# Prompt attention of a hybrid encoder step: all softmax steps of a pair of heads at the scheduling priority of the masked maximum

## Chip, cores, metric

The kernel runs on one core of one Trainium2 chip. The metric is the device time of one execution in microseconds. The kernel before took 1340.0 us, the median of 3 runs (1339.12 to 1340.05).

## What is computed

Two layers of a streaming encoder step, for a prompt of 512 rows and a sample of 32 rows behind 1024 cached positions. Both share the weights. Model width is 1024, float32. What the change concerns is mixer C of a layer: attention in which each query sees only the keys that an indexer selects. Cut to that:

```python
def sparse_attend(q, qi, wi, k_all, v_all, ki_all, limit, k_top):
    logits = jax.nn.relu(jnp.einsum('bqnd,bsd->bqns', qi, ki_all).astype(jnp.float32))
    iscore = jnp.einsum('bqn,bqns->bqs', wi.astype(jnp.float32), logits)
    admissible = jnp.arange(S)[None, :] < limit[:, None]
    iscore = jnp.where(admissible[None], iscore, -jnp.inf)
    _, sel = lax.top_k(iscore, k_top)
    ...
    s = jnp.einsum('bqhgd,bqkhd->bqhgk', qg, k_sel).astype(jnp.float32) * (HEAD_DIM ** -0.5)
    s = jnp.where(valid[:, :, None, None, :], s, -jnp.inf)
    p = jax.nn.softmax(s, axis=-1)
    o = jnp.einsum('bqhgk,bqkhd->bqhgd', p.astype(v_sel.dtype), v_sel)

def layer(...):
    z = rms_norm(x, g_mix) @ w_in
    y_a = spatial gating of za (gelu, 128-row chunks);  y_b = short gated convolution of zb
    y_c = sparse_attend of q, k, v (8 heads, 4 key heads, 64 wide; 128 keys of the prompt, 256 of the sample)
    x = x + concat(y_a, y_b, y_c) @ w_out
    x = x + square(relu(rms_norm(x) @ w_up)) @ w_down
```

## The kernel before

Everything is unrolled Python, one loop over the two layers. The prompt's rows are four blocks of 128 (b = 0 to 3), the sample's 32 rows the fifth (b = 4). A float32 product runs as three matmuls of parts (L258, L259, L260: high by high, low by high, high by low); weights are fetched on the SP queue, cast to the high part on ScalarE (L226), and the low part is the difference, on VectorE or POOL (L227).

A layer goes: indexer projection and scores, Q, K and V projections (`tok_gemm`, with `tok_gemm` of block 4 taken from small products on 32 rows, L428, and summed by L421), then attention and the other mixers, the output projection, the feed-forward part. Program order in the attention part is: the search for the sample's 256 keys (`sample_mask`: sixteen digits, each a counting pass on ScalarE, L490, small VectorE steps, and a one-column matmul, L493), `attend(0)`, then for b = 1, 2, 3 the top-128 mask (`topk_mask`: 16 rounds of MAX8, L465, and MATCH_REPLACE, L466, on 256, 384 or 512 columns; L467 turns the result into a mask) and `attend(b)`, then `mixers()`, then `attend_sample()`. Mixer A takes its V half in five products (the first uses L428 too), a gelu each on ScalarE (L908), and a spatial product each (L897).

`attend(b)` handles four pairs of heads. For a pair: two score products into PSUM tiles `psl` (L762; there are two such tiles); for each head, the masked maximum, which reads the scores and the mask and writes the masked scores and their maximum (L770, VectorE); the bias (L771, one column, VectorE); Exp with its sum (L772, ScalarE); the reciprocal (L773, one column, VectorE); the scaling (L775 on ScalarE for b below 2, L777 on VectorE otherwise). Then the probabilities are transposed (L106 into `psx` or `psd`), copied out of PSUM (L790) and multiplied by V (L794 into `pso`).

The order on each engine isn't the program's. A scheduler takes the instructions by priority, which is their place in the program plus an offset, as their inputs and buffers come free in its own reckoning. `with evac:` lowers the number of what stands in it by 2000000, `with prep:` by 1000000, so that such instructions come ahead of all others that are ready:

```python
PREP = -1000000
EVAC = -2000000

class Shift:
    def __enter__(self):
        self.tc.cur_priority += self.off
```

Each engine then runs its list strictly in that order. Before the change only L770 of the softmax steps stands in `with evac:`; the masks' rounds and the search's digits have no offset. In names such as `t_1840` the number is that of the tile; psl_1833 and psl_1834 are the scores of the second pair of heads of block 0 in layer 0, 1861 the third, 1888 the fourth, 1965, 1996, 2028 and 2059 the pairs of block 1.

Of the kernel before, what the change touches and what calls it, by code (L numbers as in the profile page):

```python
# [11 lines left out]
AF = mybir.ActivationFunctionType  # L12
ALU = mybir.AluOpType
# [42 lines left out]
def kernel(  # L56
# [7 lines left out]
    nc = tc.nc  # L64
# [16 lines left out]
    def T(n, tag=None):  # L81
        return tp.tile([128, n], F32, tag=tag or "t", name=nm("t"), bufs=TBUFS[tag or "t"])
# [4 lines left out]
    def sm(n, tag, bufs=4):  # L87
        return sp.tile([128, n], F32, tag=tag, name=nm(tag), bufs=bufs)
# [3 lines left out]
    def by_turns():  # L92
        turn[0] += 1
        return "xd"[turn[0] % 2]

    def psum(tag):
        return pp.tile([128, 512], F32, tag=tag, name=nm("ps" + tag), bufs=PBUFS[tag])

    def keep(shape, tag, dt=F32, bufs=1):
        return main.tile(shape, dt, tag=tag, name=nm(tag), bufs=bufs)  # L100

    def tr(out, in_, ident):

        if in_.dtype == F32R:
            out = out.bitcast(F32R)
        nc.tensor.transpose(out, in_, ident)  # L106
# [146 lines left out]
    def split(hi, lo, src):  # L253
        nc.scalar.copy(hi, src)
        nc.vector.tensor_tensor(lo, src, hi.bitcast(F32), op=ALU.subtract)
# [135 lines left out]
    for l in range(depth):  # L391
# [267 lines left out]
        rq = [keep([128, 8], f"rq{b}") for b in range(5)]  # L659
# [92 lines left out]
        def attend(b):  # L752

            hb, off = BLK[b]
            n = 128 * (b + 1)

            def scores(u, hh):

                p = [psum("l"), psum("l")]
                for j in range(2):  # L760
                    e = slice(64 * j, 64 * j + 64)
                    nc.tensor.matmul(p[j][:, :n], lhsT=qT[b][e, u, hh, :], rhs=kTp[e, u, :n], start=True, stop=True)  # L762
                ss2, mx, nb = sm(2, "sa", 6), sm(2, "sa", 6), sm(2, "sa", 6)
                probs = []
                for j in range(2):
                    c = 4 * u + 2 * j + hh
                    o = slice(j, j + 1)
                    t = T(n, "tt")
                    with evac:
                        nc.vector.tensor_tensor_reduce(out=t, in0=p[j][:, :n], in1=masks[b], op0=ALU.add, op1=ALU.max, scale=1.0, scalar=-3e38, accum_out=mx[:, o])  # L770
                    nc.vector.scalar_tensor_tensor(nb[:, o], mx[:, o], -1.0, rq[b][:, c:c + 1], op0=ALU.mult, op1=ALU.mult)  # L771
                    nc.scalar.activation(t, t, AF.Exp, bias=nb[:, o], scale=rq[b][:, c:c + 1], accum_out=ss2[:, o])  # L772
                    nc.vector.reciprocal(ss2[:, o], ss2[:, o])  # L773
                    if b < 2:
                        nc.scalar.activation(t, t, AF.Copy, scale=ss2[:, o])  # L775
                    else:
                        nc.vector.tensor_scalar(t, t, ss2[:, o], None, op0=ALU.mult)  # L777
                    probs.append(t)
                return probs

            def values(u, hh, probs, po):
                for k0 in range(0, b + 1, 2):
                    kn = min(2, b + 1 - k0)
                    pt = psum(by_turns() if b >= 2 else "x")
                    for k in range(kn):
                        for j in range(2):
                            tr(pt[:, (2 * k + j) * 128:(2 * k + j + 1) * 128], probs[j][:, (k0 + k) * 128:(k0 + k + 1) * 128], idn)
                    t = T(NT + NS, "pt")
                    with evac:
                        nc.scalar.copy(t[:, :kn * 256], pt[:, :kn * 256])  # L790

                    for k in range(kn):
                        for j in range(2):
                            nc.tensor.matmul(po[64 * j:64 * j + 64, hh * 128:hh * 128 + 128], lhsT=Vp[:, k0 + k, (2 * u + j) * 64:(2 * u + j + 1) * 64],  # L794
                                             rhs=t[:, (2 * k + j) * 128:(2 * k + j + 1) * 128], start=(k0 + k == 0), stop=(k0 + k == b))
                if hh == 1:
                    dst = [ys[hb][i][:, 4 + 2 * u:6 + 2 * u, off:off + 128] for i in range(2)]
                    split(dst[0], dst[1], po[:, :256].rearrange("p (h t) -> p h t", h=2))

            po = None  # L800
            for u in range(2):
                for hh in range(2):
                    probs = scores(u, hh)
                    if hh == 0:
                        po = psum("o")
                    values(u, hh, probs, po)
# [170 lines left out]
        else:  # L977
            p = psum("x")
            tr(p[:8 * depth, :128], convout.rearrange("p l c -> p (l c)"), idn)
            t = T(128)  # L980
# [46 lines left out]
        for c in range(4):  # L1027
# [12 lines left out]
            for fs in groups:  # L1040
# [5 lines left out]
                for h, n in enumerate(HALF):  # L1046
                    for f, w in zip(fs, ws):
                        p = fm_gemm(h, hs, w)
                        t = hidden[f][:, 256 * h:256 * h + n]
# [169 lines left out]
```

## Time and profile before

| | |
|---|---|
| median of the runs | 1340.0 us |
| profiled execution | 1342.9 us, span 1341.1 us |
| TensorE (PE) busy | 1299.7 us, 97% of the span |
| VectorE (DVE) busy | 1062.6 us, 79% |
| ScalarE (ACT) busy | 750.5 us, 56% |
| POOL busy | 103.8 us, 8% |
| mean granted TensorE clock | 0.981 of full |

The profile is one execution. Busy time of TensorE is the union of its pipelined matmuls. Its clock has two levels, 2.4 GHz and 1.2 GHz; the granted clock of a window is the mean over it, 1.00 where it is at full speed and 0.50 at the lower level. A wait is the idle time of an engine just before an instruction, put down to the instruction that released it. In rows of the timeline, each has its start, its duration, and how many instructions were merged.

### The profile page before, as it was taken

Reading aid. Unit: us, or ns where it says so; the run is one execution under the profiler, and the core shown is the slowest. Engines: PE = TensorE matmul, PEld = TensorE weight load, DVE = VectorE, ACT = ScalarE, POOL = GpSimd, SP = SyncE. Lnnn points to the kernel's source line nnn. Section 1 sums busy time; section 2 is a strip of 40 time slices with the busy share of each in tenths; the row PEclk is TensorE's granted clock in tenths of the full one; section 3 lists DMA queues with packets and bytes.
Section 4 is the critical chain, followed back from the end, with each engine's and each line's share of the span. In section 5 each row is a group of like instructions: output and inputs, shape, how many; then the busy total and the mean of one; then the engine's idle time right before and its main releaser. Section 6 shows DMA issues by size and latency. Waiting matters only on the chain.

```text
span 1341.1 us, 25813 instructions
## 1 busy us (share of the span) xinstructions
PE 1299.7 (97%) x10054; PEld 1212.9 (90%) x10056; DVE 1062.6 (79%) x2585; ACT 750.5 (56%) x1496; POOL 103.8 (8%) x109
## 2 busy tenths in 40 slices
PE   7898999999999999999998999999999999999998
PEld 6777887799999999999986888778999999999997
DVE  6899997567976967958989989774879588597695
ACT  5656885555535535446655579662564454463552
POOL 5215100001000000000021110000200000000000
PEclk7998999999999999999989999999999999999999
DMA  7125213032233232332211222122232423323221
GB/s 210 33 74 123 60 54 123 17 92 79 80 112 94 79 110 79 95 111 68 84 50 60 72 73 81 56 63 74 75 99 64 122 69 95 111 79 109 91 85 68
DMA packets 150802, 113.00 MB, mean 84 GB/s; under 512 B 7028, under 2 KB 147848, under 8 KB 150680
## 3 DMA queue, kind: packets, MB, share of 16 engines
q1 hardware_dynamic: 148040, 106.35, 26.4%
q0 software_dynamic: 2640, 5.01, 1.8%
q8 instruction: 79, 1.29, 0.4%
q14 instruction: 43, 0.35, 0.1%
HBM read 106.67 MB, written 4.67 MB: 83 GB/s over the span
## 4 chain that ended last, share of the span: by engine, by line
PE 81%; DVE 10%; issue 3%; DMA 3%; ACT 2%; POOL 0%; POOLq 0%; SPq 0%; DVEq 0%; ACTq 0%
PE psm L258 16%; PE psm L259 15%; PE psm L260 15%; PE psl L1086 13%; PE psd L1086 6%; PE pso L1086 3%; PE psl L762 2%; PE psx L106 2%; PE pso L794 2%; PE psd L106 1%; DVE work L623 1%; DMA ahi<-in_x_prompt_dram 1%; DMA raw<-in_w_down_dram 1%; DVE work L466 1%; PE psl L653 1%
## 5 line engine op out<-in xcount | busy, mean ns | idle before, releaser
L226 ACT CAST hi<-raw 128x1024 fp32r<-128x1024 f32 (+1 forms) x124 | 126.7, 1023 | 123.7 <-PE psm L259 71.2
L259 PE MATMUL psm<-h1lo,hi 128*128 128x288 f32 x640 | 190.5, 298 | 0.0
L258 PE MATMUL psm<-h1hi,hi 128*128 128x288 f32 x640 | 190.3, 297 | 0.0
L260 PE MATMUL psm<-h1hi,lo 128*128 128x288 f32 x640 | 189.5, 296 | 0.0
L227 DVE TENSOR_TENSOR lo<-raw,hi 128x1024 fp32r<-128x1024 f32 (+1 forms) x99 | 118.6, 1200 | 81.7 <-ACT hi L226 81.4
L258 PE MATMUL psm<-h0hi,hi 128*128 128x256 f32 x640 | 181.9, 284 | 0.0
L260 PE MATMUL psm<-h0hi,lo 128*128 128x256 f32 x640 | 181.0, 283 | 0.5 <-POOL lo L227 0.5
L259 PE MATMUL psm<-h0lo,hi 128*128 128x256 f32 x640 | 181.2, 283 | 0.0
L1086 PE MATMUL psl<-e,hi 128*128 128x272 f32 x768 | 151.4, 290 | 1.2 <-DVE x L1079 0.8
L1086 PEld LDWEIGHTS psl<-e,hi 128*128 128x128 f32 x768 | 121.6, 189 | 3.4 <-DVE x L1079 1.2
L258 PEld LDWEIGHTS psm<-h1hi,hi 128*128 128x128 f32 x640 | 120.3, 188 | 2.4 <-issue 2.3
L260 PEld LDWEIGHTS psm<-h0hi,lo 128*128 128x128 f32 x640 | 120.6, 188 | 1.0 <-POOL lo L227 0.9
L258 PEld LDWEIGHTS psm<-h0hi,hi 128*128 128x128 f32 x640 | 120.6, 188 | 0.7 <-issue 0.5
L259 PEld LDWEIGHTS psm<-h1lo,hi 128*128 128x128 f32 x640 | 120.3, 188 | 0.9 <-issue 0.8
L260 PEld LDWEIGHTS psm<-h1hi,lo 128*128 128x128 f32 x640 | 120.6, 188 | 0.4 <-issue 0.3
L259 PEld LDWEIGHTS psm<-h0lo,hi 128*128 128x128 f32 x640 | 120.5, 188 | 0.3 <-issue 0.2
L243 ACT CAST hi<-t 128x512 fp32r<-128x512 f32 x128 | 78.4, 619 | 70.5 <-PE psl L1086 24.2
L227 POOL TENSOR_TENSOR lo<-raw,hi 128x1024 fp32r<-128x1024 f32 (+1 forms) x25 | 58.1, 2325 | 734.2 <-ACT hi L226 718.0
L1086 PE MATMUL psl<-e,lo 128*128 128x272 f32 x384 | 111.0, 289 | 0.0
L243 ACT CAST hi<-raw 128x512 fp32r<-128x512 f32 x96 | 59.6, 621 | 78.6 <-PE psl L1086 47.4
L244 DVE TENSOR_TENSOR lo<-t,hi 128x512 fp32r<-128x512 f32 x128 | 87.1, 688 | 8.6 <-ACT hi L243 5.0
L1058 ACT ACTIVATE t<-t 128x544 f32<-128x544 f32 x64 | 42.2, 659 | 70.0 <-DVE t L1057 70.0
(351 smaller groups left out, 3714.4 us busy)
## 6 DMA issues: line engine op xcount, KB each, us to landing
raw<-in_w_up_dram SPq DMA_DIRECT2D x64, 512.0 KB, 4.1
raw<-in_w_down_dram SPq DMA_DIRECT2D x64, 512.0 KB, 3.5
raw<-in_w_in_dram SPq DMA_DIRECT2D x36, 512.0 KB, 4.0
raw<-in_w_out_dram SPq DMA_DIRECT2D x8, 512.0 KB, 3.5
raw<-in_w_out_dram SPq DMA_DIRECT2D x32, 128.0 KB, 3.0
raw<-in_w_in_dram SPq DMA_DIRECT2D x8, 296.0 KB, 7.0
q<-in_cache_k_dram SPq DMA_DIRECT2D x4, 512.0 KB, 4.3
h1lo<-in_cache_v_dram SPq DMA_DIRECT2D x2, 1024.0 KB, 6.2
```

Of the source, the lines that this page charges most:

```text
L106: nc.tensor.transpose(out, in_, ident)
L226: nc.scalar.copy(hi, raw)
L227: (eng or nc.vector).tensor_tensor(lo, raw, hi.bitcast(F32), op=ALU.subtract)
L243: nc.scalar.copy(hi, src)
L244: nc.vector.tensor_tensor(lo, src, hi.bitcast(F32), op=ALU.subtract)
L258: nc.tensor.matmul(out, lhsT=st[0], rhs=mv[0], start=first, stop=False)
L259: nc.tensor.matmul(out, lhsT=st[0], rhs=mv[1], start=False, stop=False)
L260: nc.tensor.matmul(out, lhsT=st[1], rhs=mv[0], start=False, stop=last)
L762: nc.tensor.matmul(p[j][:, :n], lhsT=qT[b][e, u, hh, :], rhs=kTp[e, u, :n], start=True, stop=True)
L794: nc.tensor.matmul(po[64 * j:64 * j + 64, hh * 128:hh * 128 + 128], lhsT=Vp[:, k0 + k, (2 * u + j) * 64:(2 * u + j + 1) * 64], rhs=t[:, (2 ...
L1058: nc.scalar.activation(hidden[f], hidden[f], AF.Square)
L1086: nc.tensor.matmul(p[:, :EVEN], lhsT=st[a], rhs=mv[b], start=first and (k, a, b) == (0, 0, 0), stop=(k, a) == (3, 1), skip_group_check=True)
```

## The change

Of the five steps between the scores and the probabilities of a head, four move into the `with evac:` that held the first alone. Nothing else differs.

```diff
                     with evac:
                         nc.vector.tensor_tensor_reduce(out=t, in0=p[j][:, :n], in1=masks[b], op0=ALU.add, op1=ALU.max, scale=1.0, scalar=-3e38, accum_out=mx[:, o])
-                    nc.vector.scalar_tensor_tensor(nb[:, o], mx[:, o], -1.0, rq[b][:, c:c + 1], op0=ALU.mult, op1=ALU.mult)
-                    nc.scalar.activation(t, t, AF.Exp, bias=nb[:, o], scale=rq[b][:, c:c + 1], accum_out=ss2[:, o])
-                    nc.vector.reciprocal(ss2[:, o], ss2[:, o])
-                    if b < 2:
-                        nc.scalar.activation(t, t, AF.Copy, scale=ss2[:, o])
-                    else:
-                        nc.vector.tensor_scalar(t, t, ss2[:, o], None, op0=ALU.mult)
+                        nc.vector.scalar_tensor_tensor(nb[:, o], mx[:, o], -1.0, rq[b][:, c:c + 1], op0=ALU.mult, op1=ALU.mult)
+                        nc.scalar.activation(t, t, AF.Exp, bias=nb[:, o], scale=rq[b][:, c:c + 1], accum_out=ss2[:, o])
+                        nc.vector.reciprocal(ss2[:, o], ss2[:, o])
+                        if b < 2:
+                            nc.scalar.activation(t, t, AF.Copy, scale=ss2[:, o])
+                        else:
+                            nc.vector.tensor_scalar(t, t, ss2[:, o], None, op0=ALU.mult)
```

The scheduler's order changes on every engine, in the attention part of both layers. First TensorE in layer 0, where the first two products of mixer A meet (psm_2534 is that of block 0, psm_2561 that of block 1). Before:

```order
L258 MATMUL psm_2561<-hi,h0hi_174 128x256
L259 MATMUL psm_2561<-lo,h0hi_174 128x256
L106 MATMUL psx_1852<-idr,t_1840 128x128
L260 MATMUL psm_2561<-hi,h0lo_175 128x256
L258 MATMUL psm_2561<-hi,h0hi_174 128x256
L259 MATMUL psm_2561<-lo,h0hi_174 128x256
L493 LDWEIGHTS rsum
L493 MATMUL psd_1618<-ti_1615,rsum 128x1
```

The same place now:

```order
L794 MATMUL pso_1825<-t_1855,e_41_266 64x128 x2
L106 MATMUL psx_1881<-idr,t_1868 128x128
L762 MATMUL psl_1966<-e_40_265,qT_194_823 128x256
L106 MATMUL psx_1881<-idr,t_1874 128x128
L260 MATMUL psm_2534<-hi,h0lo_175 128x256
L258 MATMUL psm_2561<-hi,h0hi_174 128x256
L259 MATMUL psm_2561<-lo,h0hi_174 128x256
L762 MATMUL psl_1996<-e_40_265,qT_194_823 128x256
L106 MATMUL psx_1907<-idr,t_1895 128x128
L762 MATMUL psl_1997<-e_40_265,qT_194_823 128x256
L260 MATMUL psm_2561<-hi,h0lo_175 128x256
```

Where one transpose of block 0's second pair and a digit of the search stood between these matmuls, the transposes of its third and fourth pairs and the scores of block 1's first and second pairs stand now; the digit comes later.

On ScalarE, the gelus of mixer A's first blocks in layer 0. Before:

```order
L908 ACT_TABLE_LOAD
L908 ACTIVATE t_2559<-psm_2534,rtok_105 128x256
L775 ACTIVATE t_1846<-t_1846,sa_1837 128x128
L772 ACT_TABLE_LOAD
L772 ACTIVATE t_1868,sa_1865<-t_1868,sa_1867,rq_188_817 128x128
L790 COPY t_1855<-psx_1852 128x256
L908 ACT_TABLE_LOAD
L908 ACTIVATE t_2586<-psm_2561,rtok_105 128x256
L490 ACTIVATE q_1562,ti_1630<-e_42_267,ti_1625,ti_1565 128x1056
```

Now:

```order
L908 ACT_TABLE_LOAD
L908 ACTIVATE t_2559<-psm_2534,rtok_105 128x256
L775 ACTIVATE t_2009<-t_2009,sa_2000 128x256
L772 ACT_TABLE_LOAD
L772 ACTIVATE t_2035,sa_2032<-t_2035,sa_2034,rq_189_818 128x256
L772 ACTIVATE t_2041,sa_2032<-t_2041,sa_2034,rq_189_818 128x256
L775 ACTIVATE t_2035<-t_2035,sa_2032 128x256
L908 ACT_TABLE_LOAD
L908 ACTIVATE t_2586<-psm_2561,rtok_105 128x256
L775 ACTIVATE t_2041<-t_2041,sa_2032 128x256
L908 ACTIVATE t_2619<-psm_2594,rtok_105 128x256
L490 ACTIVATE q_1562,ti_1614<-e_42_267,ti_1609,ti_1565 128x1056
```

Between the first two gelus stood one Exp of block 0's third pair; now two Exp of block 1's third pair with two of their scalings do. All of block 0's Exp come before the first gelu, and the digit that writes ti_1614, which came ahead of it, follows the third.

On VectorE, behind the low part of the weights of mixer A's V half, the order is now:

```order
L227 TENSOR_TENSOR lo<-raw_2519,hi 128x1024
L503 SCALAR_TENSOR_TENSOR ti_1600<-psd_1606,ti_1599 128x1
L465 MAX m_467_1961<-work_83_453 128x8
L770 ISA t_1840,sa_1838<-psl_1833,mask_346 128x128
L770 ISA sa_1838 128x1
L770 ISA t_1846,sa_1838<-psl_1834,mask_346 128x128
L770 ISA sa_1838 128x1
L771 SCALAR_TENSOR_TENSOR sa_1839<-sa_1838,rq_188_817 128x1
L499 TENSOR_SCALAR ti_1609<-ti_1600 128x1
L771 SCALAR_TENSOR_TENSOR sa_1839<-sa_1838,rq_188_817 128x1
L501 TENSOR_TENSOR ti_1611<-ti_1600,bst 128x1
L466 MATCH_REPLACE work_83_453<-m_467_1961,work_83_453 128x256
```

Before, the masked maxima of the second pair came right behind L227, and the second L771 after seven more instructions, the masked maxima of the third pair among them; now both L771 follow their maxima at once.

## Rows read from the trace of the kernel before

**Rows 1.** The page: engines' busy time, share, instructions; casts of weights with mean ns

```profile
PE 1299.7 (97%) x10054; PEld 1212.9 (90%) x10056; DVE 1062.6 (79%) x2585; ACT 750.5 (56%) x1496; POOL 103.8 (8%) x109
...
L226 ACT CAST hi<-raw 128x1024 fp32r<-128x1024 f32 (+1 forms) x124 | 126.7, 1023 | 123.7 <-PE psm L259 71.2
```

**Rows 2.** Windows: stretch, its length, busy us, then granted clock, DMA share, GB/s

```profile
core 0: us, PE busy (x) PEld busy (x) DVE busy (x) ACT busy (x) POOL busy (x), PEclk, DMA share, GB/s
...
126.50:137.00 10.50, 9.48 (x42) 7.15 (x43) 9.97 (x30) 5.36 (x11) 7.07 (x9) 0.51 0.79 171
...
764.70:772.00 7.30, 7.30 (x41) 5.68 (x42) 6.66 (x34) 4.21 (x8) 0.56 (x1) 0.53 0.57 163
...
788.50:792.50 4.00, 4.00 (x22) 3.44 (x23) 3.50 (x11) 1.55 (x3) 0.00 (x0) 0.57 0.75 184
```

**Rows 3.** TensorE's waits, 100 to 220 us: total us, times, longest us

```profile
PE psl L762 <- DVE sa L770: 2.2, 2, 1.2
...
PE psm L897 <- ACT t L908: 0.7, 1, 0.7
```

**Rows 4.** TensorE's waits, 740 to 870 us

```profile
PE psl L762 <- DVE sa L770: 4.1, 2, 2.2
...
PE psm L897 <- ACT t L908: 0.8, 1, 0.8
```

**Rows 5.** Timeline of TensorE: start, duration, line, operation, merged count, wait before

```profile
118.00 0.28 PE L259 MATMUL psm<-lo,h1hi 128*128 128x256 f32 x1
118.12 0.28 PE L260 MATMUL psm<-hi,h1lo 128*128 128x256 f32 x1
...
122.60 0.38 PE L106 MATMUL psx<-idr,t 128*128 128x128 f32 x2
122.82 0.17 PE L493 MATMUL psd<-ti,rsum 128*128 128x1 bf16 x1
122.92 0.49 PE L762 MATMUL psl<-e,qT 64*128 64x128 f32 x4
123.34 0.62 PE L428 MATMUL psm<-raw,hraw 128*32 128x256 f32 x2
...
126.54 1.00 PE L762 MATMUL psl<-e,qT 64*128 64x128 f32 x4 [1.19 <-DVE sa L770]
...
140.83 0.70 PE L762 MATMUL psl<-e,qT 64*128 64x256 f32 x4
141.46 0.65 PE L897 MATMUL psm<-wsT,t 128*64 128x128 f32 x6
```

**Rows 6.** Timeline of VectorE

```profile
127.61 3.09 DVE L720 SCALAR_TENSOR_TENSOR new<-t,rtok,sr 32x256 f32<-32x256 f32 x1
...
133.70 0.54 DVE L466 MATCH_REPLACE8 work<-m,work 128x384 f32<-128x384 f32 x1
134.16 0.68 DVE L465 MAX8 m<-e 128x8 f32<-128x512 f32 x1
```

**Rows 7.** VectorE by form, 100 to 200 us: count, busy us, mean ns

```profile
L465 DVE MAX8 m<-work 128x8 f32<-128x384 f32 x13 | 7.1, 548 | 0.0
...
L770 DVE CUSTOM_DVE_ANT_0 t<-psl,work 128x256 f32<-128x256 f32 x8 | 3.1, 416 | 0.2 <-PE psx L106 0.2
...
L771 DVE SCALAR_TENSOR_TENSOR sa<-sa,rq 128x1 f32<-128x1 f32 x20 | 2.3, 150 | 0.0
```

**Rows 8.** ScalarE by form, 100 to 200 us

```profile
L772 ACT ACT_TABLE_LOAD x7 | 9.0, 1283 | 0.1
L772 ACT ACTIVATE t<-t,sa,rq 128x256 f32<-128x256 f32 x8 | 4.7, 593 | 0.0
...
L775 ACT ACTIVATE t<-t,sa 128x256 f32<-128x256 f32 x8 | 3.8, 498 | 0.0
```

**Rows 9.** Timeline of POOL

```profile
128.04 2.37 POOL L227 TENSOR_TENSOR lo<-raw,hi 128x1024 fp32r<-128x1024 f32 x1
```

## The prediction

> **What bounds the kernel now.** The page's first part comes first: TensorE is busy 97% of the span, VectorE 79%, ScalarE 56% [rows 1]. So a step costs time where TensorE stands still or runs slowly, and an edit that only reorders VectorE and ScalarE pays by what it does to those two things. Everything the diff touches lies in the two stretches where the prompt's attention runs, about 108 to 250 us in layer 0 and 760 to 890 us in layer 1, so I read the list of TensorE's waits there, cut down to the part up to the end of the mixers' first products. In layer 0 it waited 2.2 us in two pieces of scores (L762) for the masked maximum that frees their PSUM tile, and 0.7 us for a gelu (L908) [rows 3]; in layer 1 4.1 us in two pieces for the same, and 0.8 us for the gelu [rows 4]. Then the windows: behind those waits the clock falls to its lower level, 1.2 GHz. From 126.5 to 137 us the mean grant is 0.51, from 764.7 to 772 us 0.53, from 788.5 to 792.5 us 0.57 [rows 2]. With TensorE the bound these cost 10.5 x 0.49 + 7.3 x 0.47 + 4.0 x 0.43 = 5.1 + 3.4 + 1.7 = 10.2 us. Ahead of the fall at 764.7 it had waited 2.2 us in one piece [rows 4]; ahead of the one at 126.5 1.19 us in one piece [rows 5]. So the whole of what could be won in these stretches is about 8 us of waits and 10 us of clock; what could be lost has no such limit.
>
> **What the change does.** No instruction is added or removed but a few table loads; by the two orders ScalarE's loads of activation tables go from 31 to 27. 4 x 1.283 us [rows 8] is 5.1 us of ScalarE, which lies beside TensorE's work as long as ScalarE isn't the last to arrive; I book nothing for it, and if that cover goes, part of it comes back as the gelu waits below become shorter. The Exp, the reciprocal and the scaling of a head now come ahead of everything in prep order and program order, so the softmax of blocks 0 and 1 finishes early, and the scheduler pulls the following scores and transposes forward with it. Between the first product of the mixers (L428) and the first spatial product (L897) of layer 0 TensorE had 48 GEMM matmuls with 4 transposes, 4 scores and 2 value products; it now has the same 48 with 12, 12 and 4 (layer 1: 3, 2, 2 before, 8, 6, 4 now). That is the step on which the sum rests: the same GEMM work has to cover about three times as many hand-offs between TensorE, VectorE and ScalarE.
>
> Layer 0, the pile-up. From the end of VectorE's L227 to the masked maximum of the third pair of block 1, VectorE's queue now holds 8 halves of a top-8 round on 384 columns (4 MAX8, 4 MATCH_REPLACE), 4 on 512, 2 on 256, 6 masked maxima on 128 and 4 on 256, 19 one-column operations of the softmax, 3 of the sample mask and one L467. Means are taken less 0.08, since the next starts that much earlier (133.70 to 134.16 after a row of 0.54 [rows 6]): 0.47 for MAX8 on 384 columns and 0.13 more or less for each 128 columns (0.55 against 0.68 [rows 6, 7]), MATCH_REPLACE the same and 0.07 for loading its values, a masked maximum 0.34 on 256 columns and 0.21 on 128, a one-column operation 0.07 [rows 7], L467, for which I take 0.4. The sum is 4.0 + 2.5 + 0.7 + 2.6 + 1.5 + 0.4 = 11.7 us. TensorE in the same piece has 45 matmuls at 0.12 = 5.4, 12 transposes at 0.11 = 1.3, 4 scores at 0.21 and 6 at 0.32 = 2.7 (the rows of these count each score twice), and 4 value products, taken as half a wide score, 0.16 each = 0.6 [rows 5], together 10.0 us. It can't pass VectorE's maxima, so it loses at least 1.7 us; every reciprocal also waits for an Exp on ScalarE, and in the old trace the scores that hung on such a hand-off lost 1.0 and 1.2 us at a time [rows 3]. I take 2.5, with 1.7 and 5 as the ends.
>
> Layer 0, the gelus. ScalarE is strictly in order, and the gelu of mixer block 1 now stands behind L775, a table load, two Exp on 256 columns, L775 and another load: 0.4 + 1.28 + 0.6 + 0.7 + 0.4 + 1.28 + 0.4 for itself = 5.0 us [rows 8], while TensorE has 24 matmuls of 0.12 = 2.9 us before the L897 that needs it. It waits 2.1 us; I take 2.0. The gelu of block 0 ends likewise some 0.6 us after TensorE gets there (its load and itself, 1.7 us, against three matmuls and the last two scores, 1.0). New waits of layer 0: 2.5 + 0.6 + 2.0 = 5.1; the old 2.2 + 0.7 = 2.9 go with the order that made them. **Layer 0: +2.2.**
>
> Layer 1. The same list stands before the gelu of its third block (2.0), the last gelu gets a cast of weights (L226) ahead of it, 1.0 [rows 1], and I take the pile-up as in layer 0 (2.5): 5.5. The first of the two waits of 2.2 us stays, since the first pair's maximum is where it was; 1.9 + 0.8 = 2.7 go. **Layer 1: +2.8.**
>
> The clock. I keep the 10.2 us: three stretches before, three after. Lower bound none of them but the first of layer 1 (-6.8), upper bound one more of the size of the 7.3 us one in each layer (+6.8).
>
> The sample mask's search. One of its digits (L490), which ran ahead of the first gelu, now runs behind the third. The digits that follow were spread over the rest of the mixers, where ScalarE and VectorE now have less softmax to do, so there is room to catch up: 0, with one more wait like the gelu's, 2.0 per layer, as the upper end.
>
> Queues. On SP two loads of the sample's cached keys and values change places, on POOL some stores and table builds do: 0, covered by the mixers, since the sample's attention comes after them and the tables serve the next layer. If a load were late, TensorE would still have the first half of the output projection to run.
>
> Sum: 2.2 + 2.8 = **+5.0 us**. The profiled execution took 1342.9 us for a span of 1341.1; the changed one would take 1347.9. The median of the runs is 1340.0, 2.9 lower, so I forecast **1345**.
>
> **Rivals.** A measurement of this kernel tells about 0.2%, 2.7 us, from no change; that is where I cut the three cases.
> (a) Faster. The long single waits were what the clock fell behind. In the new order each is broken into pieces of 0.2 to 0.7 us with matmuls between them. If none reaches the 1.0 us of the old ones, the stretch of layer 0 and the second of layer 1 stay at 2.4 GHz: 5.0 - 6.8 = -1.8; and if VectorE's own waits are nil and the gelu waits half, another -3.5: 1335. For it: the extra softmax work of the pile-up is work that TensorE need not wait for later. Against: the gelu wait of 2.0 us is a single piece. It decides where no wait of 1 us is left in the stretch.
> The Trainium skill's page "ScalarE: Activation LUTs" (section "Table sets: the hidden batching unit") tells to batch activations by table set, which this change does; by that rule alone the four loads would be won, some 5 us. Here ScalarE's share [rows 1] says that it isn't the bound.
> (b) No change. The order only moves waits: new ones as large as the old. TensorE's work is the same: 1340.
> (c) Much slower. In the old trace VectorE's L720 took 3.09 us on a tile for which 0.4 is due [rows 6], just while POOL ran its own L227 (128.04, 2.37 us) [rows 9]. If one of the moved one-column operations (L771, with two operands in SBUF) meets that POOL operation, the whole pile-up is held for up to 2.4 us more per layer, and a long wait brings a further stretch at 1.2 GHz: 5.0 + 4.8 + 3.4 = +13: 1353.
> The Trainium skill's page "SBUF — State Buffer" (section "Who interferes with whom") states this lock for a VectorE instruction with two SBUF inputs against a GpSimd one that reads SBUF. By that rule the masked maximum, which reads PSUM and one SBUF tile, is safe and L771 is not, so it speaks against moving L771. The trace agrees for L720; for L771 no row shows it.
>
> **How the numbers follow.** Forecast 0.48, (a) 0.22, (b) 0.20, (c) 0.10. Of the forecast's 0.48 some 0.06 lies under 2.7 us. Slower 0.42 + 0.10 = 0.52, within 0.2% 0.20 + 0.06 = 0.26, faster 0.22. The range takes in (a) down to a little below its 1335 and (c) to a little above 1353: 1333 to 1355. The forecast's own is 1341 to 1350.
>
> **What would show it.** Right: in the new list of TensorE's waits L897 behind L908 grows to 2 us or more per layer, and L762 behind L770 becomes many pieces; the scores of block 1 all run before or around the first L897; the low-clock stretches are about as long. Wrong: a granted clock of 1.0 from 120 to 150 us (then (a)); a gelu wait under 1 us; or a loss that lies after 200 us, at the sample mask, which I put at nothing.

## The result, and the profile after

The changed kernel took 1361.7 us in the median of 4 runs (1356.9 to 1364.7), beside 1340.0 for the kernel before: a ratio of 1.0157, interval 1.0141 to 1.0172. Repeated beside other kernels it took 1355.3 (1353.0 to 1358.4, 4 runs) beside 1339.1: 1.0119, 1.0101 to 1.0137. So it is slower, as forecast, but by 16 to 22 us instead of 5, and outside the range.

The profiled execution took 1364.7 us for a span of 1362.8, 21.7 more than the span before. The page's line of engines, which answers to [rows 1]:

```profile
PE 1313.3 (96%) x10056; PEld 1219.7 (89%) x10056; DVE 1066.0 (78%) x2585; ACT 748.2 (55%) x1492; POOL 104.2 (8%) x109
```

TensorE is busy 13.6 us longer with the same matmuls, so most of the loss isn't waiting. The windows, which answer to [rows 2], say what it is (length, busy us, then granted clock, DMA share, GB/s):

```profile
130.00:155.00 25.00, 25.00 (x90) 16.64 (x84) 14.59 (x69) 13.55 (x36) 4.88 (x8) 0.50 0.25 50
155.00:175.00 20.00, 16.21 (x126) 11.76 (x127) 18.63 (x58) 16.18 (x30) 3.44 (x3) 1.00 0.23 59
175.00:183.00 8.00, 8.00 (x37) 5.30 (x37) 6.20 (x26) 7.51 (x14) 2.16 (x4) 0.57 0.07 16
783.00:790.00 7.00, 6.62 (x38) 4.71 (x38) 5.93 (x30) 5.08 (x14) 0.00 (x0) 0.51 0.55 152
...
806.00:814.00 8.00, 7.57 (x33) 5.35 (x34) 5.74 (x32) 5.27 (x15) 0.51 (x1) 0.57 0.35 90
```

In layer 0 one stretch at 1.2 GHz begins at 127.8 us and lasts to 155.1, and another follows from about 175.5 to 182.4; before there was one of 10 us. Added up from windows of 1 us, the missing grant (time times 1 less the granted clock) costs layer 0 17.1 us instead of 5.1, layer 1 6.8 instead of 5.1. The waits, which answer to [rows 3] and [rows 4] (100 to 220 us, then 740 to 870 us; total us, times, longest us):

```profile
PE psl L762 <- DVE sa L770: 4.3, 2, 2.6
PE psm L897 <- ACT t L908: 1.4, 1, 1.4
...
PE psl L762 <- DVE sa L770: 5.8, 4, 2.9
PE psm L897 <- ACT t L908: 2.2, 3, 1.5
```

For a balance I take each layer from its first L421 (69.2 us before) to the first product of the feed-forward part (L1086, 355.9 us), the missing grant in it, and the sum of TensorE's list of waits, all in us:

| profiled execution | layer 0: length, clock, waits | layer 1: length, clock, waits |
|---|---|---|
| before | 286.7, 5.1, 7.3 | 282.8, 5.1, 7.4 |
| changed | 304.1, 17.1, 11.0 | 287.3, 6.8, 10.9 |
| changed, repeated (after_again) | 297.5, 10.2, 10.8 | 285.8, 5.1, 10.3 |

The first execution lost 17.4 + 4.5 = 21.9 us in these two stretches, which is the whole difference of the spans: 13.7 of clock, 7.2 of waits, 1.0 of the rest. The repeated one lost 13.8: 5.1 of clock, 6.4 of waits, 2.3 of the rest. The waits agree from one execution to the other; the clock doesn't. The mean clock over the runs does tell the kernels apart: span times (1 - mean clock) is 33 us on average over the 8 runs of the changed kernel (clock 0.971 to 0.979) and 21.5 us over 81 runs of the kernel before (0.979 to 0.988). So about 11.5 us of the loss are clock and 7 are what is left of the span without it.

The rest in layer 0 (1.7 us in the first execution, 2.2 in the repeat) is neither wait nor clock. Before the change two scores of 256 columns in a row took TensorE 0.63 us together (140.83 to 141.46 [rows 5]). In the repeat one alone takes 0.62 us, from its start to that of the next operation:

```profile
138.88 0.70 PE L762 MATMUL psl<-e,qT 64*128 64x256 f32 x2
139.50 0.33 PE L106 MATMUL psx<-idr,t 128*128 128x128 f32 x1
```

The change breaks such pairs up. Of the 32 prompt scores of layer 0, 8 ran alone before and 18 do now, in both executions. Taken up to the next operation, less waits, with time at 1.2 GHz counted half, the scores took 16.7 us of TensorE before, 18.5 in the first execution and 18.8 in the repeat: 1.8 and 2.1 us more.

### The profile page after: what moved, and what is told of

It is laid out like the page before. It is cut to its first block, busy times and chain, and to the rows that moved or that the text cites. A ratio compares the mean times of both kernels' runs of the same rounds, so it can differ in the third digit from the quotient of the medians.

```text
span 1362.8 us, 25801 instructions
## 1 busy us (share of the span) xinstructions
PE 1313.3 (96%) x10056; PEld 1219.7 (89%) x10056; DVE 1066.0 (78%) x2585; ACT 748.2 (55%) x1492; POOL 104.2 (8%) x109
## 5 line engine op out<-in xcount | busy, mean ns | idle before, releaser
L226 ACT CAST hi<-raw 128x1024 fp32r<-128x1024 f32 (+1 forms) x124 | 126.7, 1024 | 126.2 <-PE psm L259 70.5
L227 DVE TENSOR_TENSOR lo<-raw,hi 128x1024 fp32r<-128x1024 f32 (+1 forms) x99 | 119.1, 1205 | 81.9 <-ACT hi L226 81.7
L1086 PE MATMUL psl<-e,hi 128*128 128x272 f32 x768 | 151.3, 289 | 1.3 <-ACT hi L243 0.6
L1086 PEld LDWEIGHTS psl<-e,hi 128*128 128x128 f32 x768 | 121.7, 189 | 3.4 <-ACT e L254 1.0
L227 POOL TENSOR_TENSOR lo<-raw,hi 128x1024 fp32r<-128x1024 f32 (+1 forms) x25 | 58.1, 2327 | 745.8 <-ACT hi L226 729.7
L1086 PE MATMUL psl<-e,lo 128*128 128x272 f32 x384 | 111.0, 289 | 0.0
```

Source lines behind the costliest of these rows:

```text
L226: nc.scalar.copy(hi, raw)
L227: (eng or nc.vector).tensor_tensor(lo, raw, hi.bitcast(F32), op=ALU.subtract)
L1086: nc.tensor.matmul(p[:, :EVEN], lhsT=st[a], rhs=mv[b], start=first and (k, a, b) == (0, 0, 0), stop=(k, a) == (3, 1), skip_group_check=True)
```

## The experiments

**Is it the kernel's own, and which blocks make it?** The first repeats the kernel, the others keep `with evac:` for some blocks only, by this edit at each of the four steps (here for block 0):

```diff
-    evac = Shift(tc, EVAC)
+    evac, plain, soon, top = [Shift(tc, i) for i in (EVAC, 0, PREP, 2 * EVAC)]
...
-                        nc.scalar.activation(t, t, AF.Exp, ...)
+                    with (evac if b == 0 else plain): nc.scalar.activation(t, t, AF.Exp, ...)
```

after_again:

> The changed kernel once more, unaltered, on the chip of the other runs of this call, for the spread of its executions and their mean clock. If the loss is the kernel's own (crowding or lock): 1355 to 1365, mean clock 0.970 to 0.978 in every execution, against 0.981 or more of the kernel before. If the first four executions were an accident of where the clock stood: some executions below 1350.

b0_only:

> The four steps stand in the evacuation priority for block 0 alone, for both layers. Crowding (my theory: the softmax of blocks 0 and 1 is pulled into the mixers' V products, so that TensorE's list there mixes scores, transposes and products, and the clock, once fallen, stays at 1.2 GHz from 127 to 156 us): the scores of block 1 go back behind the mixers, the low stretch of layer 0 is 11 us as before or at most 18, time 1338 to 1348. Lock (rival: L771 held by POOL's L227 for 2.3 us starts it all): the moved L771 of block 0 still meets POOL, so most of the loss stays, 1352 to 1362. Gelu (rival: the gelu behind two Exp of block 1 costs it): block 1's Exp are behind again, 1338 to 1343.

b1_only:

> The four steps stand in the evacuation priority for block 1 alone. Crowding: block 0 runs late as before and block 1 can't come ahead of it, because they share the score tiles and the tile of transposes; little is pulled forward, 1338 to 1348. Lock: the L771 that meets POOL's L227 is block 0's, which isn't moved, so no loss: 1338 to 1343. Gelu: the Exp of block 1 stand ahead of a gelu somewhere, 1342 to 1350.

b23_only:

> The four steps stand in the evacuation priority for blocks 2 and 3 alone, where the scaling is VectorE's. All three theories place the loss ahead of 160 us in layer 0 and ahead of 815 us in layer 1, where these blocks don't run: 1337 to 1343.

b01_only:

> The four steps stand in the evacuation priority for blocks 0 and 1, as in the change, but not for blocks 2 and 3. Crowding (the scores and transposes of block 1 stand among the products while the clock is low, and keep it low): all of it is here, 1353 to 1363 with a stretch of 20 us or more at 1.2 GHz in layer 0. If blocks 2 and 3 are needed for the loss (none of my theories says so): 1338 to 1346.

Measured: after_again 1355.3; b0_only 1342.3 (ratio 1.0024, 1.0014 to 1.0035); b1_only 1342.7 (1.0017, 1.0006 to 1.0027); b23_only 1344.3 (1.0030, 1.0018 to 1.0041); b01_only 1353.3 (1.0109, 1.0089 to 1.0129). Blocks 0 and 1 together cost what the whole change costs, each alone 2 us. The lock's 1352 to 1362 for b0_only was missed, though the second L771 of block 0 did take 2.32 us there beside POOL's L227; b1_only fits all three theories and doesn't tell them apart. b01_only has crowding's time but not its stretch of 20 us or more: layer 0 shows three stretches, of 10, 3 and 7 us, as in the repeat. Blocks 2 and 3 alone cost 4 us, which none of the theories had (they said 1337 to 1343). Lone scores account for most of that: in the profiled execution of b23_only layer 0 is 3.1 us longer, and its scores take 2.1 us more (12 run alone), those of layer 1 1.0 more.

b0_only also shows the clock at work. TensorE's list is that of the changed kernel, matmul for matmul, up to the second pair of block 1's scores, and the first wait is the same (2.75 us against 2.62). The windows of b0_only:

```profile
124.50:135.00 10.50, 10.25 (x41) 7.27 (x41) 8.37 (x33) 3.60 (x12) 6.66 (x8) 0.51 0.73 159
135.00:152.00 17.00, 17.00 (x134) 13.40 (x132) 14.82 (x61) 14.65 (x29) 1.71 (x2) 1.00 0.01 4
```

Here the clock is back after 10 us; in the first execution of the changed kernel it stayed down for 27. The list ahead of that point doesn't decide it, then. What follows in the list differs, products in b0_only and block 1's scores in the changed kernel, but that doesn't decide it alone either: the repeat, u_part, b01_only and noload (below) have the same TensorE list as the first execution up to the first L897, and in all four the clock was back after 10 us. TensorE's timeline of the changed kernel there (start, duration, merged count; the rows of L762 count each score twice):

```profile
127.68 0.74 PE L762 MATMUL psl<-e,qT 64*128 64x128 f32 x2 [2.62 <-DVE sa L770]
...
140.74 1.22 PE L762 MATMUL psl<-e,qT 64*128 64x256 f32 x2
141.89 0.47 PE L106 MATMUL psx<-idr,t 128*128 128x128 f32 x1
142.02 0.56 PE L260 MATMUL psm<-hi,h0lo 128*128 128x256 f32 x1
142.38 0.41 PE L258 MATMUL psm<-hi,h0hi 128*128 128x256 f32 x1
142.59 0.41 PE L259 MATMUL psm<-lo,h0hi 128*128 128x256 f32 x1
142.93 1.22 PE L762 MATMUL psl<-e,qT 64*128 64x256 f32 x2
```

From 137 to 151 us six such scores of 256 columns (L762) stand alone between the products, each with some 1.1 us of TensorE at this clock (140.74 to 141.89). By the trace TensorE was busy 25.0 of 25.0 us (the first row of the windows above), so it waited for nothing; VectorE, busy 14.6 us, waited for TensorE. The other run with a long stretch is gelu_top (below), whose list has block 1's scores at this place too (length, busy us, clock, DMA share, GB/s):

```profile
127.70:148.20 20.50, 20.50 (x77) 13.97 (x76) 14.06 (x53) 10.59 (x25) 6.73 (x9) 0.50 0.33 71
```

In these two the clock fell 0.08 and 0.34 us after the wait had ended; in the four that came back after 10 us it fell between 0.53 us before the wait's end and 0.02 after. No run shows whether that decides it.

**Is it POOL holding VectorE?** In the first profiled execution the lock of rival (c) had come true. VectorE's timeline, then POOL's:

```profile
124.53 0.72 DVE L718 TENSOR_SCALAR rq<-sr,rtok 32x8 f32<-32x8 f32 x1
125.16 0.48 DVE L720 SCALAR_TENSOR_TENSOR new<-t,rtok,sr 32x256 f32<-32x256 f32 x1
125.67 1.23 DVE L227 TENSOR_TENSOR lo<-raw,hi 128x1024 fp32r<-128x1024 f32 x1
126.93 0.16 DVE L503 SCALAR_TENSOR_TENSOR ti<-psd,ti 128x1 f32<-128x1 f32 x1
127.01 0.42 DVE L465 MAX8 m<-work 128x8 f32<-128x256 f32 x1
127.34 0.27 DVE L770 CUSTOM_DVE_ANT_0 t<-psl,mask 128x128 f32<-128x128 f32 x1
...
128.22 2.32 DVE L771 SCALAR_TENSOR_TENSOR sa<-sa,rq 128x1 f32<-128x1 f32 x1
```

```profile
128.19 2.34 POOL L227 TENSOR_TENSOR lo<-raw,hi 128x1024 fp32r<-128x1024 f32 x1
```

The second L771 took 2.32 us on one column, while POOL ran L227. This is the lock of the Trainium skill's page "SBUF — State Buffer", section "Who interferes with whom"; the trace agrees, here for L771 as before for L720. Two kernels give the low part of the U half's weights to VectorE (`w_feat(C_U + 128 * fb)` instead of `w_feat(C_U + 128 * fb, nc.gpsimd)`):

u_dve (the changed kernel):

> The whole change, with the low part of the weights of mixer A's U half taken by VectorE instead of POOL, so that no POOL operation on SBUF runs beside the moved L771. Lock: the piece of 2.3 us in L771 goes and the long stretch at 1.2 GHz with it, 1340 to 1350. Crowding: the stretch at 1.2 GHz stays at 20 us or more, 1355 to 1365 (VectorE has 4 x 1.2 us more to do). Gelu: unchanged, 1357 to 1365.

old_u_dve (the kernel before):

> The kernel before, with the low part of the weights of mixer A's U half taken by VectorE instead of POOL: the control for the same edit on the changed kernel. Lock: VectorE's L720, 3.09 us beside POOL there, falls to 0.5 us; one wait of 1 us in layer 0 goes, the stretch at 1.2 GHz stays (the wait ahead of it is not of POOL): 1336 to 1341. If VectorE's 4 x 1.2 us of added work reaches TensorE: 1341 to 1346.

Measured: 1340.0 (1.0000, 0.9990 to 1.0009) and 1339.2 (1.0000, 0.9988 to 1.0013). u_dve lies in the lock's range (1340 to 1350): the whole loss was gone, and for a while the lock was my theory. But u_dve has another order on all engines, so two kernels followed in which POOL computes only a small part of that low part (the rest is left out), and whose order on TensorE, VectorE and ScalarE is row for row that of the changed kernel and of the kernel before:

```diff
-            (eng or nc.vector).tensor_tensor(lo, raw, hi.bitcast(F32), op=ALU.subtract)
+            (eng or nc.vector).tensor_tensor(lo[:, some, some], raw[:, some, some], hi.bitcast(F32)[:, some, some], op=ALU.subtract)
...
-            return load_w(w_in[l, :, c0:c0 + 128], 8, 128, eng)
+            return load_w(w_in[l, :, c0:c0 + 128], 8, 128, eng, slice(0, 8) if eng else slice(None))
```

u_part:

> The whole change; POOL computes the low part of the weights of mixer A's U half for 64 of 1024 columns only (the rest of that low part is left out), so POOL's L227 there takes 0.2 us instead of 2.4, and the order on TensorE, VectorE and ScalarE stays that of the changed kernel, row for row. Lock (VectorE's small operations held by POOL make the maxima late, and TensorE's waits and falls of the clock follow from it): L771, L509 and L159 take 0.2 us, the waits of 1.7 us at 167 us in layer 0 and of 2.9 us in layer 1 go, and with them one stretch at 1.2 GHz in each layer: 1340 to 1348. Crowding alone (the order is enough): 1352 to 1361, as the changed kernel.

old_u_part:

> The kernel before with the same cut of POOL's work, and its own order kept row for row: the control. Lock: VectorE's L720 falls from 3.1 to 0.5 us and L718 of layer 1 from 2.1 to 0.2; the waits of 0.98 us in layer 0 and 1.93 us in layer 1 go: 1334 to 1338. Crowding alone: 1337 to 1340, since POOL's operation isn't the bound.

Measured: u_part 1348.4 (1.0068, 1.0048 to 1.0089), old_u_part 1333.5 (0.9950, 0.9935 to 0.9965). Both kernels gain 6 to 7 us (from 1355.3 and 1339.5), so without POOL's operation the change still costs 1.0068 / 0.9950 = 1.0119, what the repeat gave with it. u_part lies between what was expected of the lock (1340 to 1348) and of crowding (1352 to 1361); with its control it says that the lock is dear, but hardly part of the difference. In layer 0 it did nothing to the changed kernel: L771 takes 0.28 us at most in u_part, and windows and waits are those of the repeat (u_part; layer 0 in the first three rows, layer 1 in the fourth):

```profile
126.50:137.00 10.50, 10.26 (x42) 7.07 (x43) 6.05 (x33) 3.49 (x12) 5.25 (x9) 0.52 0.84 179
...
153.50:157.50 4.00, 4.00 (x24) 3.77 (x25) 2.75 (x12) 2.28 (x4) 0.32 (x1) 0.57 0.00 0
...
167.50:174.50 7.00, 7.00 (x29) 4.39 (x28) 6.24 (x26) 6.33 (x15) 2.08 (x4) 0.52 0.07 19
...
782.00:830.00 48.00, 44.35 (x357) 36.31 (x356) 44.04 (x165) 39.69 (x80) 5.58 (x11) 1.00 0.27 74
```

```profile
PE psl L762 <- DVE sa L770: 4.3, 2, 2.6
PE psm L897 <- ACT t L908: 1.8, 1, 1.8
...
PE psl L762 <- DVE sa L770: 3.5, 4, 2.2
PE psm L897 <- ACT t L908: 2.1, 3, 1.5
```

In layer 1 it had held another operation, L159 of the K norms, two 32 x 12 operands in SBUF (VectorE, changed kernel):

```profile
801.97 2.24 DVE L159 SCALAR_TENSOR_TENSOR sr<-sr,sr 32x12 f32<-32x12 f32 x1
```

A score's wait of 2.85 us and a fall of the clock at 807 us came behind that; both are gone in u_part (layer 1: clock 3.4, waits 8.1). The kernel before had the like: L718 took 2.12 us there, a wait of 1.93 us and a fall at 788.8 us came behind it, and both are gone in old_u_part. So of the 15 us between the repeat and u_dve some 7 are what u_part gains too, and the other 8 come with u_dve's order: with the same first wait (2.61 us) and two for the gelu (1.7 and 1.0) its clock fell once in layer 0, for 10 us.

**Is it ScalarE's gelu?** Its chain in the repeat (ScalarE, then the two waits of TensorE that came ahead of falls):

```profile
146.93 0.47 ACT L908 ACTIVATE t<-psm,rtok 128x256 f32<-128x256 f32 x1
147.30 0.50 ACT L775 ACTIVATE t<-t,sa 128x256 f32<-128x256 f32 x1
147.81 1.28 ACT L772 ACT_TABLE_LOAD   x1
149.11 0.61 ACT L772 ACTIVATE t<-t,sa,rq 128x256 f32<-128x256 f32 x1
...
149.71 0.59 ACT L772 ACTIVATE t<-t,sa,rq 128x256 f32<-128x256 f32 x1
...
150.58 0.51 ACT L775 ACTIVATE t<-t,sa 128x256 f32<-128x256 f32 x1 [0.19 <-DVE sa L773]
151.11 1.28 ACT L908 ACT_TABLE_LOAD   x1
152.40 0.47 ACT L908 ACTIVATE t<-psm,rtok 128x256 f32<-128x256 f32 x1
```

```profile
152.93 0.66 PE L897 MATMUL psm<-wsT,t 128*64 128x128 f32 x8 [1.77 <-ACT t L908]
...
167.08 1.09 PE L762 MATMUL psl<-e,e 64*128 64x384 f32 x2 [1.67 <-DVE sa L770]
```

From one gelu to the next (146.93 to 152.40) ScalarE does what the prediction listed: L775, load, two Exp, L775, load. (The first L775 scales t_2009, of block 1's second pair; only the other is of the third pair, as the Exp are.) TensorE waits 1.77 us, and at 154.0 the clock falls; the other wait, for block 2's masked maximum, stands ahead of the fall at 167.7. The windows of the repeat:

```profile
126.50:137.00 10.50, 9.74 (x40) 6.93 (x41) 7.28 (x32) 3.49 (x12) 6.73 (x9) 0.51 0.75 172
137.00:153.50 16.50, 14.73 (x99) 10.62 (x98) 15.49 (x62) 14.38 (x35) 1.50 (x3) 1.00 0.06 12
153.50:157.50 4.00, 4.00 (x22) 3.89 (x21) 2.69 (x9) 2.69 (x5) 0.30 (x1) 0.57 0.00 0
...
167.50:174.50 7.00, 7.00 (x29) 4.57 (x29) 6.06 (x24) 5.96 (x13) 2.07 (x4) 0.51 0.07 18
```

Two edits: the gelu's `with evac:` becomes `with Shift(tc, 2 * EVAC):` (gelu_top), or its function `AF.Exp` (noload), which leaves no loads between it and the softmax.

gelu_top:

> The whole change, with the gelu of mixer A's V half (L908) at twice the evacuation priority, ahead of the softmax. Gelu (my prediction's term): the waits of L897, 1.8 us in layer 0 and 2.1 in layer 1, go to 0.5 or less each, with the stretch at 1.2 GHz behind the first: 1348 to 1355. Lock or crowding: the waits move to the scores, 1352 to 1362.

noload:

> The whole change, with an Exp in the place of mixer A's gelu of the V half, so that ScalarE needs no loads of tables between it and the softmax (that gelu is left out). If ScalarE's delay of the gelu brings the second and third falls of the clock in layer 0: the waits of L897 (1.8 and 2.1 us) and the stretches behind them go, 1342 to 1350. If the mix of scores and products on TensorE does: 1350 to 1358, with the stretches in layer 0 still over 8 us of loss.

Measured: gelu_top 1352.6 (1.0085, 1.0066 to 1.0104), noload 1350.1 (1.0089, 1.0066 to 1.0111). gelu_top fits both of its expectations, noload stands on the line between its two, and both intervals overlap the repeat's (1.0101 to 1.0137). With gelu_top the gelu waits are nearly gone (0.2 us in layer 1), but TensorE waits 10.1 us in layer 0 all the same, now for weights: 1.7 for POOL's L227, 1.3 for ScalarE's L226. With noload TensorE's list is that of the changed kernel up to the first L897, no wait for the gelu is left, and neither fall behind it comes:

```profile
126.50:137.50 11.00, 10.35 (x41) 7.25 (x41) 8.87 (x34) 3.50 (x12) 6.65 (x8) 0.53 0.74 166
...
153.00:157.00 4.00, 4.00 (x33) 2.83 (x34) 3.29 (x16) 2.90 (x7) 0.42 (x1) 1.00 0.00 0
...
167.00:175.00 8.00, 8.00 (x55) 5.85 (x55) 6.90 (x27) 5.63 (x12) 0.00 (x0) 1.00 0.22 63
```

```profile
PE psl L762 <- DVE sa L770: 2.6, 1, 2.6
```

Layer 0's clock and waits are as in the kernel before (5.1 and 7.3); its length, 293.2, is 4.3 less than the repeat's, not 8.6. Most of the rest went into scores: behind the first L897 noload has an order of its own, 24 scores of layer 0 run alone, and they take 21.7 us at full clock, 2.9 more than in the repeat. Layer 1 hardly changed. So in these two executions 8.6 us of clock and waits in layer 0 hang on the gelu behind two Exp and its loads, the later two falls among them; between the medians it is 4 to 5 us. The page "ScalarE: Activation LUTs" of the Trainium skill, section "Table sets: the hidden batching unit", tells to batch by table set. The change did so (31 loads to 27) and it didn't pay: the four loads fewer came with a gelu that ended 5.5 us after the one before it.

**Which steps?**

act_only (`with evac:` at L772 and L775 alone):

> Only ScalarE's steps, the Exp and the scaling of blocks 0 and 1, stand in the evacuation priority; VectorE's bias and reciprocal stay as before. If ScalarE's part makes the loss (the gelu behind Exp and table loads): 1350 to 1360. If the loss needs VectorE's one-column steps too, since an Exp can't start ahead of its bias: 1339 to 1346.

dve_only (at L771, L773 and L777 alone):

> Only VectorE's steps, the bias, the reciprocal and the scaling of blocks 2 and 3, stand in the evacuation priority. If ScalarE's part makes the loss: 1337 to 1344. If VectorE's part does: 1350 to 1360.

Measured: 1347.7 (1.0059, 1.0047 to 1.0071) and 1341.7 (1.0010, 1.0001 to 1.0019). act_only lies between its two expectations: ScalarE's steps carry half of the loss, with a gelu wait of 2.3 us in layer 0; VectorE's alone cost 1 to 2 us; the rest needs both.

**More work for TensorE in the wait.** after_fill30 adds, ahead of the first L428 of the mixers and at the priority of `with evac:`, 30 times

```python
nc.tensor.matmul(p[:, :256], lhsT=hs[0][0][:, 0, 0:128], rhs=hs[0][0][:, 1, 0:256], start=True, stop=True)
```

> The whole change; ahead of the first product of the mixers' V half TensorE gets 30 more matmuls of 256 columns in the evacuation priority, whose result is overwritten (3.6 us per layer of added work at full clock, a product of 128 by 256 that nothing uses). They lie where TensorE waited 2.6 us for the masked maximum. Clock (the fall at 127 us comes from that wait, and the rest from not coming back among the scores): no fall in layer 0 or a short one, so -13 or more of clock, +1 to +3 of added work not covered: 1343 to 1352. Lock: L771 is still held by POOL, VectorE's maxima are late all the same, the wait moves behind the added matmuls and they are paid in full: 1360 to 1372.

Measured: 1367.7 (1.0217, 1.0200 to 1.0234), worse than the changed kernel. The added matmuls moved the scheduler's order; the wait became 4.7 us in one piece and the gelu waits of layer 0 5.2. The time lies in the lock's range (1360 to 1372), but no L771 was held here: they took 0.15 us and stood behind POOL's L227, which ended at 130.05. On the clock it tells little: the missing grant was 5.1 us in layer 0 and 11.9 in layer 1.

**Versions meant to beat both.** u_dve_gelu has the edits of u_dve and of gelu_top; old_u0_dve is the kernel before with `w_feat(C_U + 128 * fb, (None, nc.gpsimd)[fb])`, so that VectorE takes the one tile whose subtraction on POOL met L720 and L718.

u_dve_gelu:

> Both edits on the changed kernel: the low part of the U half on VectorE, and the gelu at twice the evacuation priority; a try at a version that beats both kernels. With the first alone 1340.0, of which 4.3 us are waits for the gelu: if these go, 1334 to 1338; if they only move, 1338 to 1342.

old_u0_dve:

> The kernel before, with VectorE in the place of POOL for the first of the two tiles of the U half's low part in each layer (the one that met L720 and L718); a try at a version faster than both. Without POOL's work it took 1333.5; VectorE has 2 x 1.2 us more to do: 1334 to 1338. If those 1.2 us lie ahead of a maximum that TensorE waits for, 1338 to 1341.

Measured: u_dve_gelu 1345.5 (1.0044, 1.0028 to 1.0060); old_u0_dve 1337.5 (0.9984, 0.9974 to 0.9994). The first missed its ranges (1334 to 1342). The second beats the kernel before by 2 us; the 6 us that old_u_part shows aren't had. Its order is a new one again: 18 scores of layer 0 run alone in place of 8, for 3.2 us of TensorE.

## Right and wrong, step by step

- **Slower, and where:** right. The loss lies in the two stretches named, most of layer 0's ahead of 190 us.
- **The gelus:** right in the main. Booked were 0.6 + 2.0 us in layer 0 and 2.0 + 1.0 in layer 1; L897 waited 1.4 to 1.8 us in one piece (the 0.6 didn't come) and 2.1 to 2.2. "2 us or more per layer" holds in layer 1 alone.
- **The pile-up:** too small, and wrong in shape. For L762 2.5 us were booked in layer 0 and 2.5 + 2.2 in layer 1; it waited 4.3 and 5.8, and not in many pieces, but in 2.6 and 1.7 us in layer 0 and up to 2.9 in layer 1. I counted VectorE's list from the end of its L227. In the new order L718 and L720 stand ahead of that L227, and L503 and a MAX8 behind it (the timeline above), so the first masked maximum ended at 127.61 us in place of 126.48; 0.67 us of this is that TensorE's last L421 ahead of it, too, ran later (122.84 in place of 122.17). And TensorE reached the score sooner, at 125.06 in place of 125.35, since no transpose waits among its L428 any more. So the 1.19 us [rows 5] became 2.62. Before the change (TensorE, then VectorE):

```profile
124.45 0.33 PE L106 MATMUL psx<-idr,t 128*128 128x128 f32 x1 [0.50 <-ACT e L728]
126.19 0.29 DVE L770 CUSTOM_DVE_ANT_0 t<-psl,mask 128x128 f32<-128x128 f32 x1
```

Behind that first wait TensorE waited for none of block 1's maxima in layer 0. The sum of 10.0 us against VectorE's 11.7 took a matmul at 0.12 us, its time at full clock, though the clock's own term had 10 us of this stretch at 1.2 GHz, where one takes 0.21 (142.38 to 142.59). And it took a score at half a pair's time, 0.32 us, where one alone takes 0.62.
- **The old waits that go:** the 1.0 us of layer 0 was no hand-off by way of an Exp, as I read it. It stood behind the L720 that POOL held, and is gone in old_u_part, where L762 waits 1.2 us in layer 0 and 2.2 in layer 1, in one piece each.
- **Waits together:** booked +2.2 and +2.8; the balance gives +3.5 to +3.7 and +2.9 to +3.5.
- **The clock:** wrong, and this is the step that failed. I wrote "I keep the 10.2 us: three stretches before, three after", with one more stretch per layer as the upper bound. The missing grant is 23.9 us in the first execution and 15.3 in the repeat, for the two layers, and over all runs the clock costs about 11.5 us more than before. I took the length of a stretch, some 10 us in layer 0, as given, though no row showed what ends one; and I let the waits cost only themselves, though the fall behind each was in [rows 2] and [rows 5]. With the repeat's two new falls (1.7 and 3.4 us in layer 0) the sum would have been about +10, and with 2 us for the lone scores about +12; the repeat lost 13.8. The range was also narrower than its own terms: 1345 with the upper ends of layer 0's pile-up (+2.5), of the clock (+6.8) and of the search (+4.0) is 1358, not 1355.
- **Rival (c):** its lock took place in the first execution (in the repeat the longest L771 took 0.90 us), and its 1353 lies nearest to what was measured, but the lock isn't the reason: u_part shows layer 0 unchanged without it. Its further stretch at 1.2 GHz did come.
- **Booked at nothing:** the search's digits (L106 behind L528 waits 0.9 us before and after) and the table loads held. For the queues no wait points the other way.

What is shown: the order of blocks 0 and 1 together makes the loss (b01_only), and not the lock (u_part with old_u_part); most of it is clock (the mean clock of the runs), the rest waits and, in layer 0, scores that run alone. That the gelu chain brings two of the falls rests on one execution of noload. Only argued: that the mix of scores and products kept the clock down for 27 us; four executions with the same list came back after 10. Open: what decides between the two, why a wait is followed by a fall in one order and not in another, and the last us of what blocks 2 and 3 alone cost.

## What to carry to other kernels

Where the bound engine's clock falls behind its waits, price a wait with the fall that its own trace shows behind it, and give a stretch at the low clock no fixed length. Raising the priority of work that isn't late pulls its consumers forward as well: here the scores of the next block, into the one stretch where the products had to cover everything else. A pair of scores that an order breaks up cost twice the time here; count in the new list which stand alone. And to test one operation, keep the order: an edit that lets the scheduler lay out the program anew (u_dve) can remove the loss for another reason.

## What the runs showed of the hardware

From run to run the changed kernel varied by 7.8 us in its first four runs (1356.9 to 1364.7) and by 5.3 in the repeat, together with its mean clock (0.978 to 0.971 in the first four); the kernel before varied by 1.5 in the four runs beside it (1339.1 to 1340.6), but by 7.4 over the 81 others (1336.6 to 1344.0). A wait of 1.7 us stood ahead of a fall in the repeat and not in u_dve, and in act_only one of 2.3 us had no fall behind it. Two scores of 256 columns in a row took TensorE 0.63 us, and one alone 0.62. And two POOL subtractions of 2.4 us per layer, on an engine busy 8% of the span, cost the kernel before 6 us (old_u_part).
